# A hybrid diffusion step on one core: a new order for late loads, weight splits, query evictions and the first conv products

## The chip, the core and the metric

One core of a Trainium2 chip runs the whole step. TensorE (PE) multiplies and transposes; VectorE (DVE), ScalarE (ACT) and GpSimd (POOL) do the rest; SyncE (SP) issues nearly all DMAs. The metric is the device time of one execution in microseconds (us): the median of several runs, lower is better.

## The reference

One layer, for 512 latent tokens and 128 context tokens of width 1024, all in float32. Cut to what matters here:

```
mod = silu(cond) @ w_ada + b_ada                     # six parts: sh1 sc1 g1 sh2 sc2 g2
h = rms(x, norm_mix) * (1 + sc1) + sh1
q, k, v, gb, gc, u = split(h @ w_in)                 # 512, 128, 128, 512, 512, 512 columns
q, k = rms per head of 64; latent tokens get rotary positions
attn = softmax(q k^T / 8) v                          # latent queries: 128 cached keys and 512 latent keys in one softmax;
                                                     # context queries: the 128 context keys
y_conv = gb * conv3(gc * u)
x = x + g1 * (concat(rms(attn), rms(y_conv)) @ w_out)
x = x + g2 * ((silu(gate) * up) @ w_down)            # gate, up = split(h2 @ w_gate_up), h2 the second modulated norm
```

The outputs are both token sets and the context's keys and values.

## The kernel before

Every float32 matrix product is three products of split operands: a value is rounded to a high part ("hi", `wh`, `hH`) and the rest is kept as a low part ("lo", `wl`, `hL`); `mm3` issues hi*hi, hi*lo and lo*hi. Splitting a weight tile of 128x1024 takes one ACT instruction for the high part and one DVE instruction for the low part.

**First stage, an order written out by hand.** `P1SEQ` is a string of steps. DVE, ACT, POOL, SP and PE each execute their share of its instructions in the order of the string (each engine by itself; an engine waits only where it needs another's result). Eight rounds k = 0 to 7 go over the eight blocks of 128 of the model width. The letters:

- `rT`, `sT`, `xT`: sum of squares and the inverse root (POOL), scaling, and PE transposes of token tile T (T = 4 is the context); `eTix` evicts half a transposed tile on ACT (`a`) or DVE (`d`).
- `ak`, `bk`, `mk`: the products that give sc1 and sh1 of block k (line 385, from `af` tiles of w_ada), their copy from PSUM (DVE, line 430), and a small product (line 437) whose evictions on DVE give the scale and shift `modA`, `modB`.
- `hk0`, `hk1`: the modulated block `hF`, rounded to `hH` and `hL`, for latent and context tokens.
- `qkT`: the query products of block k and token tile T, three PE instructions.
- `w`, `l`: the ACT and the DVE half of the split of the next loaded w_in tile (lines 526 and 533).
- `c`: constants; `d`: dummy products; `p` (`rows2_load`): five small DMAs on POOL with gains and conv weights; `v1`: a PE transpose of those rows; `R` (`rope_tables`): two DMAs of 128 KB on POOL with the rotary tables, and POOL products for them.

`LOADS` gives SP's order in this stage: `x` a token tile, `A` the four 256 KB loads of w_ada for one block (`af`, buffers for two blocks), `W` the next 512 KB tile of w_in (`wf`, three buffers; the split results have four). `wf` tiles come in the order of `plan`: four for queries, two for keys and values, then the conv tiles for gc, u and gb of each of four column groups, between which lie the w_ada tiles (`aw`) that later stages need.

After the string come two DMAs of the cached keys and values (`ck`, `cv`, 64 KB each) and five copies of the query sums out of PSUM (`qraw`): the context's on DVE, the latent tiles' on ACT. These are not in the hand-written order; a planner with a cost model places them and everything in the next stages on ACT, DVE, POOL and SP. PE's order stays as the program states it.

**Second stage, phase 1.** `SEQ` is the order of PE's work: `kT` key and value products of tile T (`kv_mm`, 24 PE instructions and the per-head norm `head_norm`), `c0` splits the cached keys and values, `CT`/`KT` transpose split keys, `qT`/`QT` norm and transpose queries, `a`, `t`, `o` are the context's attention (scores, transposes, output), `Sn.h`, `Tn.g`, `On.g` the same for 16 units of latent attention, `r` sums of squares. `F1` runs one filler step: 84 steps, in fixed order, of the four conv column groups (six steps each for gc, u and gb, of nine or six PE instructions) and of the rest of the modulation (`ada`). `W(key)` loads ahead: it issues the loads up to a few places past the tile that it is asked for.

**Later stages** (output projection, feed-forward) are not touched.

Of the kernel before, what the change touches and what calls it, by code (L numbers as in the profile page):

```python
# [9 lines left out]
F32 = mybir.dt.float32  # L10
F32R = mybir.dt.float32r
AF = mybir.ActivationFunctionType
# [3 lines left out]
P = 128  # L16
# [3 lines left out]
NT = 5  # L20
TOK = NT * P
CTX = 4
HD = 64
NH = 8
NKV = 2
# [5 lines left out]
EPS = 1e-6  # L31
CG = 32
P1SEQ = ('d8 r0 s0 x0 r1 s1 r2 e00d x1 s2 e01d r3 v0 d4 x2 s3 e20a a0 e10d b0 e11d e21d x3 m0 d4 w e30a h00y l n0 '
# [4 lines left out]
XB = 3  # L38
SEQ = ('k1 c0 q4 k4 C0 k0 K4 Q4 q0 a0 F1 k2 a1 K0 t0 k3 t1 o0 K1 F1 Q0 o1 K2 F1 K3 F1 S0.0 F1 F1 S0.1 '
# [10 lines left out]
GCUT = [0, 6, 12, 17, 22]  # L50
GB = 3
SOP = [20, 0]
# [2 lines left out]
FEND = 2  # L55
AOP = 9
NPLAIN = 2
QEV = '00001'
PPO = ''
RSP = 0  # L60
G2P = -300
# [23 lines left out]
AHEAD = 3  # L85
OSQ = 2
AFB = 4
LOADS = 'xxxxAWxAAWAAWAAAWWWW'
O_Q, O_K, O_GB, O_GC, O_U = 0, 512, 768, 1280, 1792


def build(ctx, tc, x_prompt, x_sample, c, cache_k, cache_v, c_ctx, norm_mix, norm_ffn, w_ada, b_ada,
# [3 lines left out]
    act, dve, pool, pe, sp = nc.scalar, nc.vector, nc.gpsimd, nc.tensor, nc.sync  # L96
# [16 lines left out]
    def close_pool(name):  # L113
        pools[name][0].__exit__(None, None, None)
# [5 lines left out]
    def T(tag, shape, dt=F32, bufs=1):  # L120
        seq[0] += 1
        return pools[where.get(tag, "A")][1].tile(list(shape), dt, tag=tag, bufs=bufs, name=f"{tag}_{seq[0]}")

    def PB(shape=(P, 512), dt=F32, tag="t"):
        seq[0] += 1
        if kept.get(tag):
            w = kept[tag].pop()
            n = 1
            for y in shape[1:]:
                n *= y  # L130
            w = w[:, :n] if tag != "s" else w
            if tag != "s" and len(shape) > 2:
                names = "abc"[:len(shape) - 1]
                w = w.rearrange("p (" + " ".join(names) + ") -> p " + " ".join(names), **dict(zip(names, shape[1:])))
            return w
        return pools["psum"][1].tile(list(shape), dt, tag=tag, bufs=pbufs[tag], name=f"p{tag}_{seq[0]}")
# [52 lines left out]
    def plan(key, src, ph=0, ring="w", gain=None):  # L189
        place[key] = len(order)  # L190
        order.append([key, src, ph, ring, gain, None])
# [60 lines left out]
    def load_next(later=False):  # L252
        load(order[stream_at[0]], later)
        stream_at[0] += 1
# [19 lines left out]
    ada_steps = [(sec, j, h) for sec, j in ADA for h in range(4)]  # L274
    for n, (off, ct) in enumerate(CONV + [(None, 0)]):
        if off is not None:
            plan(("conv", off, ct), wi[:, :, off + ct * P:off + (ct + 1) * P])
        for sec, j, h in ada_steps[2 * n:2 * n + 2 if off is not None else None]:
            col = sec * D + j * 512
            plan(("ada", sec, j, h), wa[:, 2 * h:2 * h + 2, col:col + 512], 1, "a")  # L280
    for j in range(2):
# [17 lines left out]
    for gi, grp in enumerate(GROUPS):  # L299
# [5 lines left out]
        for j in range(2):  # L305
            for i0 in range(0, len(grp), 2):
                n = len(grp[i0:i0 + 2])
# [37 lines left out]
    def x_load():  # L345
        xt = T("x", (P, D), F32, NT)
        sp.dma_start(xt, x_dram[len(xs)])
        xs.append(xt)

    def ada1_next(n):  # L350
        for _ in range(n):
            next(loads, None)
# [5 lines left out]
    pre_order.__enter__()  # L358
    for a in LOADS:
        if a == "A":  # L360
            ada1_next(3)
        elif a == "W":
            load_next(True)
        else:
            x_load()
    ones = T("ones", (P, P))
    dve.memset(ones, 1.0)
    neghalf = T("neghalf", (P, 16))
# [132 lines left out]
    qacc = [PB(tag="c")]  # L501
# [40 lines left out]
    def rows2_load():  # L542
        for nm, g in (("q", q_norm), ("k", k_norm)):
            pool.dma_start(gain_rows[nm], g[0].partition_broadcast(P))
        pool.dma_start(rows2[0:4, :], attn_out_norm[0].rearrange("(r q) -> r q", q=P))
        pool.dma_start(rows2[4:8, :], conv_out_norm[0].rearrange("(r q) -> r q", q=P))
        pool.dma_start(rows2[8:20, :], conv_w[0].rearrange("w (r q) -> (w r) q", q=P))
# [3 lines left out]
    def rope_tables():  # L551

        rt = T("oz", (P, 2, NL, HD))
        rc, rs_ = rt[:, 0], rt[:, 1]
        pool.dma_start(rc, rope_c.rearrange("(t p) d -> p t d", p=P))
        pool.dma_start(rs_, rope_s.rearrange("(t p) d -> p t d", p=P))
        for nm in "qk":
            gb_ = gain_rows[nm]
            tab = T("tab", (P, 2, NL, HD), F32, 2)
            cg, sg = tab[:, 0], tab[:, 1]  # L560
            pool.tensor_tensor(cg, rc, gb_.unsqueeze(1).to_broadcast([P, NL, HD]), ALU.mult)
            s4 = sg.rearrange("p t (a b c) -> p t a b c", a=2, b=2)
            r4 = rs_.rearrange("p t (a b c) -> p t a b c", a=2, b=2)
            g4 = gb_.rearrange("p (a b c) -> p a b c", a=2, b=2)
            for b in range(2):
                for a in range(2):
                    pool.tensor_tensor(s4[:, :, a, b], r4[:, :, a, b],
                                       g4[:, a, 1 - b].unsqueeze(1).to_broadcast([P, NL, 16]), ALU.mult)
            gains.append(gb_)
            tabs.append((cg, sg))  # L570

    steps = {"r": x_norm, "s": x_scale, "c": late_consts, "w": w_hi, "l": w_lo, "p": lambda i: rows2_load(), "x": xT_do,
             "v": lambda i: (vec_do, vec2_do)[i](), "m": ada1_mod, "a": ada1_mm, "b": ada1_res, "d": spin,
             "n": h_rest, "R": lambda i: rope_tables()}
    in_pre[0] = True
    for x in P1SEQ.split():
        k = int(x[1:2] or 0)
# [7 lines left out]
            steps[x[0]](k)  # L585
    pre_order.__exit__(None, None, None)
    in_pre[0] = False
    ck = T("ck", (P, NKV, HD))
    sp.dma_start(ck, cache_k[0, 0])
    cv = T("cv", (P, NKV, HD))  # L590
    sp.dma_start(cv, cache_v[0, 0])
    qraw = [None] * NT
    for t in (CTX, 0, 1, 2, 3):
        qraw[t] = T("of", (P, 512), F32, NT)
        if QEV[t] == '1':
            dve.tensor_copy(qraw[t], qacc[t])
        else:
            act.activation(qraw[t], qacc[t], AF.Copy)
    close_pool("B0")
    open_pool("B2", "left", "vt KA KB VS qT pr ph pl osq c25 aw es")  # L600
    phase[0] = 1
# [203 lines left out]
    of = [None] * NT  # L805
# [137 lines left out]
    def rms_of(t):  # L943
        if t == CTX or t >= 0:
# [5 lines left out]
             "a": ctx_s, "t": ctx_t, "o": ctx_o, "r": att_rms}  # L950
    for x in SEQ.split():
        if "." in x:
            n, i = (int(y) for y in x[1:].split("."))
# [113 lines left out]
    for j in range(2):  # L1067
        cols = slice(j * 512, (j + 1) * 512)
        for n, t in enumerate(TORD):
            cc = 1 if t == CTX else 0  # L1070
            c0 = t * P + (2 if t == CTX else 0)
# [229 lines left out]


tile_hymba = with_exitstack(build)

_INS = ["x_prompt", "x_sample", "c", "cache_k", "cache_v", "c_ctx", "norm_mix", "norm_ffn", "w_ada", "b_ada",
# [44 lines left out]
```

## Time and profile before

| | |
|---|---|
| Median of three runs | 761.21 us (760.87 to 762.34) |
| Profiled execution | 763.84 us, of which the span of instructions 762.1 us |
| PE, DVE, ACT, POOL busy | 742.6, 553.9, 368.0, 43.8 us |
| Mean granted PE clock | 0.995 |
| HBM traffic | 79.68 MB read, 2.75 MB written |
| First stage | up to about 63 us |
| Phase 1 | about 63 to 272 us |

Lines of the profile read: start, duration (us), engine, source line, operation, written tile <- read tiles, shapes, count, and in brackets the idle time before it and what ended it. "Waits" lines read: who waited, for whom, us in total, times, longest. The chain lists start, duration and what held up the end. Windows list the busy time of each engine in a stretch, then the clock granted to PE (1.00 is full), the DMA engines' mean share and GB/s.

### The profile page before, as it was taken

Reading aid. Unit: us, or ns where it says so; the run is one execution under the profiler, and the core shown is the slowest. Engines: PE = TensorE matmul, PEld = TensorE weight load, DVE = VectorE, ACT = ScalarE, POOL = GpSimd, SP = SyncE. Lnnn points to the kernel's source line nnn. Section 1 sums busy time; section 2 is a strip of 40 time slices with the busy share of each in tenths; the row PEclk is TensorE's granted clock in tenths of the full one; section 3 lists DMA queues with packets and bytes.
Section 4 is the critical chain, followed back from the end, with each engine's and each line's share of the span. In section 5 each row is a group of like instructions: output and inputs, shape, how many; then the busy total and the mean of one; then the engine's idle time right before and its main releaser. Section 6 shows DMA issues by size and latency. Waiting matters only on the chain.

```text
span 762.1 us, 11916 instructions
## 1 busy us (share of the span) xinstructions
PE 742.6 (97%) x4612; PEld 666.7 (87%) x4612; DVE 553.9 (73%) x1005; ACT 368.0 (48%) x713; POOL 43.8 (6%) x75
## 2 busy tenths in 40 slices
PE   7899999999999999999999999999999999999997
PEld 5578888989999887899998789998889998899986
DVE  5456997676666798779979678884577866788653
ACT  5336867666656434765652135553125541255410
POOL 2401300111000110100000000000000000000000
PEclk9999999999999999999999999999999999999999
DMA  9966133522432463031335223233113132122312
GB/s 290 289 199 196 36 118 91 171 94 90 156 108 90 132 245 115 1 111 56 89 106 180 83 60 107 69 99 112 54 55 108 60 111 82 57 87 81 111 56 83
DMA packets 101389, 84.52 MB, mean 111 GB/s; under 512 B 3502, under 2 KB 81650, under 8 KB 101332
## 3 DMA queue, kind: packets, MB, share of 16 engines
q1 hardware_dynamic: 100980, 83.39, 35.5%
q8 instruction: 36, 0.59, 0.3%
q0 software_dynamic: 352, 0.37, 0.2%
q14 instruction: 21, 0.17, 0.1%
HBM read 79.68 MB, written 2.75 MB: 108 GB/s over the span
## 4 chain that ended last, share of the span: by engine, by line
PE 84%; DVE 6%; DMA 5%; ACT 2%; issue 1%; SPq 0%; POOL 0%; DVEq 0%; ACTq 0%
PE pf L157 17%; PE pf L156 17%; PE pf L155 17%; PE pc L703 3%; PE pc L705 3%; PE pc L704 3%; PE po L860 2%; PE ps L817 2%; PE pc L385 2%; PE ph L155 2%; PE ph L157 2%; PE ph L156 2%; PE pt L843 2%; DMA af<-in_w_ada_dram 2%; DMA es<-t 1%
## 5 line engine op out<-in xcount | busy, mean ns | idle before, releaser
L151 ACT ACTIVATE wh<-wf 128x512 fp32r<-128x512 f32 (+1 forms) x69 | 56.6, 821 | 85.6 <-PE pf L157 62.0
L157 PE MATMUL pf<-wh,gT 128*128 128x512 f32 (+1 forms) x225 | 88.3, 393 | 0.0
L156 PE MATMUL pf<-wl,gT 128*128 128x512 f32 (+1 forms) x225 | 87.7, 390 | 0.0
L155 PE MATMUL pf<-wh,gT 128*128 128x512 f32 (+1 forms) x225 | 87.6, 389 | 0.0
L152 DVE TENSOR_TENSOR wl<-wf,wh 128x1024 fp32r<-128x1024 f32 (+1 forms) x35 | 40.6, 1161 | 28.7 <-ACT wh L151 23.6
L703 PE MATMUL pc<-hH,wh 128*128 128x320 f32 x192 | 61.1, 318 | 0.0
L705 PE MATMUL pc<-hH,wl 128*128 128x320 f32 x192 | 59.4, 309 | 0.0
L704 PE MATMUL pc<-hL,wh 128*128 128x320 f32 x192 | 59.3, 309 | 0.0
L156 PEld LDWEIGHTS pf<-wl,gT 128*128 128x128 f32 x225 | 42.2, 188 | 10.3 <-DVE wl L152 0.2
L155 PEld LDWEIGHTS pf<-wh,gT 128*128 128x128 f32 x225 | 42.2, 188 | 9.8 <-ACT wh L151 0.2
L155 PE MATMUL pf<-T,wh 128*128 128x320 f32 x160 | 49.6, 310 | 0.9 <-ACT u L1180 0.5
L157 PEld LDWEIGHTS pf<-wh,gT 128*128 128x128 f32 x225 | 42.3, 188 | 9.4
L155 PE MATMUL pf<-T,wl 128*128 128x320 f32 x160 | 49.4, 309 | 0.0
L156 PE MATMUL pf<-T,wl 128*128 128x320 f32 x160 | 49.4, 309 | 0.0
L157 PE MATMUL pf<-T,wh 128*128 128x320 f32 x160 | 49.4, 309 | 0.0
L156 PE MATMUL pf<-T,wh 128*128 128x320 f32 x160 | 49.4, 309 | 0.0
L157 PE MATMUL pf<-T,wl 128*128 128x320 f32 x160 | 49.4, 309 | 0.0
L155 PE MATMUL pf<-B,wl 128*128 128x320 f32 x152 | 47.1, 310 | 0.0
L157 PE MATMUL pf<-B,wl 128*128 128x320 f32 x152 | 47.0, 309 | 0.0
L156 PE MATMUL pf<-B,wl 128*128 128x320 f32 x152 | 46.9, 309 | 0.0
L1259 DVE TENSOR_TENSOR dm<-pf,g 128x512 f32<-128x512 f32 (+1 forms) x41 | 27.7, 675 | 23.4 <-PE pf L157 23.3
L155 PE MATMUL pf<-B,wh 128*128 128x320 f32 x136 | 42.2, 310 | 1.5 <-DVE cu L1209 1.5
(304 smaller groups left out, 2046.5 us busy)
## 6 DMA issues: line engine op xcount, KB each, us to landing
wf<-in_w_gate_up_dram SPq DMA_DIRECT2D x44, 512.0 KB, 3.9
aw<-in_w_ada_dram SPq DMA_DIRECT2D x24, 512.0 KB, 4.5
wf<-in_w_down_dram SPq DMA_DIRECT2D x20, 512.0 KB, 3.4
wf<-in_w_in_dram SPq DMA_DIRECT2D x18, 512.0 KB, 5.7
af<-in_w_ada_dram SPq DMA_DIRECT2D x32, 256.0 KB, 6.7
x<-in_x_sample_dram SPq DMA_DIRECT2D x8, 512.0 KB, 6.1
wf<-in_w_out_dram SPq DMA_DIRECT2D x8, 512.0 KB, 4.3
wf<-in_w_ada_dram SPq DMA_DIRECT2D x8, 512.0 KB, 3.7
```

What stands on the lines that cost most here:

```text
L151: act.activation(hi, src, AF.Copy)
L152: dve.tensor_tensor(lo, src, f32(hi), ALU.subtract)
L155: pe.matmul(out, lh, rh, start=start, stop=False, skip_group_check=more)
L156: pe.matmul(out, lh, rl, start=False, stop=False, skip_group_check=more)
L157: pe.matmul(out, ll, rh, start=False, stop=stop, skip_group_check=more)
L385: pe.matmul(out[CG * g:CG * (g + 1)], cp[:, k], w, start=(k < 4), stop=(k >= KD - 4), skip_group_check=True)
L703: pe.matmul(acc, wh[:, k], hH[k][:, c0:c0 + n], start=(k == 0), stop=False)
L704: pe.matmul(acc, wh[:, k], hL[k][:, c0:c0 + n], start=False, stop=False)
L705: pe.matmul(acc, wl[:, k], hH[k][:, c0:c0 + n], start=False, stop=(k == KD - 1))
L817: pe.matmul(s2[:, g, :320], q, kk[:, v, P + g * 320:P + (g + 1) * 320], start=(i == 0), stop=(i == 1))
L843: pe.transpose(tp[:, i, h], u[3][h][:, kt * P:(kt + 1) * P], ident)
L1259: dve.tensor_tensor(dm, ps[:, :n], g2[cc][:, oc], ALU.mult)
```

## The change

- The DMAs of `ck` and `cv` move into the hand-written order, behind all of `LOADS`, on SP.
- `LOADS` gets an eighth `W`: the first u tile of the conv is loaded and split in the first stage too. In `plan` the w_ada tiles move one conv tile later, so that this tile is next.
- In `P1SEQ` the splits `w l` from the fourth on come earlier: the fourth in round 6 ahead of `q51` (it was behind `b7`), the fifth ahead of `q54` (it was behind `q61`), the sixth behind `q61`, the seventh behind `q64`, and the new eighth at the end.
- `a3 b3` move behind `q13 q14`, and `q20` ahead of `m3`. `p0` moves from round 1 to round 2, `R` from round 4 to round 5, `v1` from round 2 to the end of round 5.
- The five query copies become steps `E0` to `E4` between the last query products, in the hand-written order; before, the context's copy stood first in the program.
- In `SEQ` one filler moves between `K4` and `Q4`, others move ahead around `Q0`, `K2`, `K3` and `S0`, and one each is taken out behind `T9.1` and `T14.1`. The number of fillers is the same, 84.

```
-         'r4 q01 e31d s4 p0 q02 a1 x4 b1 e40d m1 h01x h10 q00 a2 b2 h11 q04 m2 w e41a q03 l q10 h20 q11 q12 h21 a3 b3 q13 q14 '
-         'm3 h30 h31 q20 q21 a4 b4 q22 q23 c0 q24 v1 m4 h40 h41 R q30 q31 a5 b5 w l q32 q33 q34 '
-         'm5 h50 h51 q40 q41 a6 b6 q42 q43 q44 m6 h60 h61 q50 q51 a7 b7 w l q52 q53 q54 '
-         'm7 h70 h71 q60 q61 w l q62 q63 q64 w l w l q70 q71 q72 q73 q74')
+         'r4 q01 e31d s4 q02 a1 x4 b1 e40d m1 h01x h10 q00 a2 b2 h11 q04 m2 w e41a q03 l q10 h20 q11 q12 h21 q13 q14 a3 b3 '
+         'q20 m3 h30 h31 q21 a4 b4 q22 q23 c0 p0 q24 m4 h40 h41 q30 q31 a5 b5 w l q32 q33 q34 '
+         'm5 h50 h51 q40 q41 a6 b6 q42 q43 R q44 m6 h60 h61 q50 w l q51 a7 b7 q52 q53 w l q54 v1 '
+         'm7 h70 h71 q60 q61 w l q62 q63 q64 w l q70 E0 q71 E1 q72 E2 q73 E3 q74 E4 w l')
...
-SEQ = ('k1 c0 q4 k4 C0 k0 K4 Q4 q0 a0 F1 k2 a1 K0 t0 k3 t1 o0 K1 F1 Q0 o1 K2 F1 K3 F1 S0.0 F1 F1 S0.1 '
+SEQ = ('k1 c0 q4 k4 C0 k0 K4 F1 Q4 q0 a0 F1 k2 a1 K0 t0 k3 t1 o0 K1 F1 Q0 o1 F1 K2 F1 K3 F1 F1 S0.0 F1 S0.1 '
...
-       'T8.1 F1 S9.1 T8.2 O8.0 F1 O8.1 S10.0 F1 F1 T9.0 O8.2 T9.1 F1 F1 F1 O9.0 T9.2 S10.1 F1 r1 O9.1 '
+       'T8.1 F1 S9.1 T8.2 O8.0 F1 O8.1 S10.0 F1 F1 T9.0 O8.2 T9.1 F1 F1 O9.0 T9.2 S10.1 F1 r1 O9.1 '
...
-       'T14.1 F1 F1 F1 T14.2 F1 F1 O14.0 O14.1 T15.0 F1 O14.2 F1 T15.1 T15.2 F1 F1 O15.0 O15.1 F1 O15.2')
+       'T14.1 F1 F1 T14.2 F1 F1 O14.0 O14.1 T15.0 F1 O14.2 F1 T15.1 T15.2 F1 F1 O15.0 O15.1 F1 O15.2')
...
-LOADS = 'xxxxAWxAAWAAWAAAWWWW'
+LOADS = 'xxxxAWxAAWAAWAAAWWWWW'
...
-        for sec, j, h in ada_steps[2 * n:2 * n + 2 if off is not None else None]:
+        for sec, j, h in ada_steps[2 * n - 2:2 * n if off is not None else None] if n else ():
...
+    ck, cv = (T(x, (P, NKV, HD)) for x in ("ck", "cv"))
+    sp.dma_start(ck, cache_k[0, 0])
+    sp.dma_start(cv, cache_v[0, 0])
...
+    def q_evict(t):
+        qraw[t] = T("of", (P, 512), F32, NT)
+        if t == CTX:
+            dve.tensor_copy(qraw[t], qacc[t])
+        else:
+            act.activation(qraw[t], qacc[t], AF.Copy)
```

The lines behind the loop over `P1SEQ` that issued `ck`, `cv` and the five copies go away with `QEV`, and the step table gets `"E": q_evict`.

More of the change, by code (lines that the diff above doesn't have):

```diff
@@ L57 @@
 NPLAIN = 2
-QEV = '00001'
 PPO = ''
@@ L570, in rope_tables @@
             tabs.append((cg, sg))
+    qraw = [None] * NT
+    def q_evict(t):
[4 more added lines that the diff above has]
+            act.activation(qraw[t], qacc[t], AF.Copy)
     steps = {"r": x_norm, "s": x_scale, "c": late_consts, "w": w_hi, "l": w_lo, "p": lambda i: rows2_load(), "x": xT_do,
              "v": lambda i: (vec_do, vec2_do)[i](), "m": ada1_mod, "a": ada1_mm, "b": ada1_res, "d": spin,
-             "n": h_rest, "R": lambda i: rope_tables()}
+             "n": h_rest, "E": q_evict, "R": lambda i: rope_tables()}
     in_pre[0] = True
@@ L587, in build @@
     in_pre[0] = False
[L588 to L598, printed above, removed]
     close_pool("B0")
```

## The prediction

> **What bounds the kernel now.** First the page's head, then who TensorE (PE) waited for, then the stretches those waits lie in.
>
> ```profile
> span 762.1 us, 11916 instructions
> PE 742.6 (97%) x4612; PEld 666.7 (87%) x4612; DVE 553.9 (73%) x1005; ACT 368.0 (48%) x713; POOL 43.8 (6%) x75
> ```
> ```profile
> PE pc L385 <- DMA af<-in_w_ada_dram: 2.4, 1, 2.4
> PE pt L647 <- ACT osq L639: 1.6, 1, 1.6
> ...
> PE pt L683 <- ACT qT L684: 1.0, 1, 1.0
> PE ps L817 <- ACT pr L825: 0.8, 1, 0.8
> ```
> PE is busy for 742.6 of 762.1 us. The change adds and removes no product, so it can only win PE's idle time or the clock. Four large waits lie where it edits. The windows (PE, PEld, DVE, ACT, POOL busy, granted clock, DMA share, GB/s) show what the first two cost besides:
>
> ```profile
> 27.50:31.00 3.50, 1.20 (x11) 0.31 (x9) 1.16 (x3) 0.74 (x1) 1.57 (x4) 1.00 1.14 268
> 31.00:34.40 3.40, 3.15 (x13) 1.98 (x14) 0.42 (x1) 0.00 (x0) 2.30 (x7) 0.50 1.05 300
> ...
> 68.50:71.90 3.40, 1.52 (x12) 1.19 (x11) 2.62 (x9) 1.80 (x6) 2.52 (x2) 1.00 0.56 157
> 71.90:75.30 3.40, 3.40 (x19) 3.40 (x18) 2.96 (x10) 1.58 (x5) 0.75 (x2) 0.51 0.10 31
> ```
> ```profile
> 86.00:92.00 6.00, 5.43 (x43) 4.78 (x42) 5.80 (x19) 5.97 (x20) 1.25 (x2) 1.00 0.19 53
> ...
> 98.00:104.00 6.00, 5.21 (x35) 3.91 (x35) 5.38 (x11) 4.49 (x9) 0.00 (x0) 1.00 0.56 152
> ...
> 110.00:272.00 162.00, 161.44 (x1152) 146.16 (x1151) 112.35 (x222) 100.34 (x202) 15.63 (x25) 1.00 0.37 118
> ```
> After each of the two long waits PE runs one stretch at half clock (0.50, 0.51). In 110 to 272 us PE idles 0.56 us, so a gain made before 105 us is carried to the end. In 86 to 104 VectorE (DVE) is itself over 90% busy (5.80 and 5.38 of 6): what is won before it may be capped there.
>
> **Change, part 1: the fourth round of the first stage (27 to 41 us).**
>
> ```profile
> 22.05 9.07 DMA af<-in_w_ada_dram
> ```
> ```profile
> 27.43 0.40 PE L156 MATMUL ps<-wl,hH 128*128 128x512 f32 x1
> 27.66 0.40 PE L157 MATMUL ps<-wh,hL 128*128 128x512 f32 x1
> ...
> 31.25 1.08 PE L385 MATMUL pc<-af,cp 128*32 128x256 f32 x8 [2.37 <-DMA af<-in_w_ada_dram]
> ...
> 35.10 0.47 PE L155 MATMUL ps<-wh,hH 128*128 128x512 f32 x1
> ```
> ```profile
> 19.05 0.47 SPq L589 DMA_DIRECT2D ck<-in_cache_k_dram  x1
> 19.57 0.43 SPq L591 DMA_DIRECT2D cv<-in_cache_v_dram  x1
> 20.13 9.74 SPq L324 DMA_DIRECT2D af<-in_w_ada_dram  x8
> ```
> *Loads.* The cached keys and values stand on SP's queue just ahead of the modulation weights that a3 waits for. They are 2 x 64 KB = 131 kB; at the 268 to 300 GB/s of the windows that is 0.45 us. So the last a3 load lands at 31.12 - 0.45 = 30.67. Bounds: 0 (SP's buffers come free no sooner) and 1.08 (the issue time 19.05 to 20.13).
> *a3 behind q13 q14.* Six products start 0.23 apart (27.43, 27.66): 1.40 us of work that needs only round 1, moved into the 2.37 us wait. Idle left: 2.37 - 1.40 - 0.45 = 0.52, a gain of 1.85 (1.4 to 2.37).
> *Clock.* From 31.25 to 35.10, 3.85 us, PE does half of a3, q13, q14 and m3 at half clock; at the warm spacing this is about 0.5 + 0.4 of switching + 1.4 + 0.35 = 2.65. With q13 q14 ahead, the window 27.5 to 31 holds 1.20 + 1.40 = 2.6 busy of 3.5 and I take it to stay warm: 1.2 (0 to 1.3). Sum 3.05; I take 3.0, bounds 1.4 and 3.7. Next late is the load of round 4, some 1 MB or 3.6 us behind a3's at those rates, at 34.3 at the latest; PE wants it at about 33.4, and its first half comes sooner: up to 0.5 of the 3.7 may go there.
> *p0, R, v1.* p0 and R issue seven DMAs, all on POOL.
>
> ```profile
> 21.91 0.79 POOL L555 DMA_DIRECT2D oz<-rope_c_dram  x1
> ```
> R stood behind h41 in the order, yet POOL issued it at 21.91: each engine follows the order by itself, and nothing but the r steps stands before p0 on POOL. Moving p0 and R leaves POOL's order as it is: nothing changes, and their 336 KB stay in the way of a3's load (bounds 0 and -1.1 us, their bytes at 300 GB/s). v1 is one transpose moved; PE pays it in either place: 0.
>
> **Part 2: splits one round sooner (52 to 60 us).**
>
> ```profile
> 53.00 1.04 ACT L526 ACTIVATE wh<-wf 128x1024 fp32r<-128x1024 f32 x1
> ...
> 53.87 0.42 DVE L430 COPY res<-pc 128x256 f32<-128x256 f32 x1
> 54.20 1.22 DVE L533 TENSOR_TENSOR wl<-wf,wh 128x1024 fp32r<-128x1024 f32 x1
> ...
> 56.65 0.82 ACT L474 ACTIVATE hF<-xT,modB,modA 128x512 f32<-128x512 f32 x1 [2.60 <-DVE modB L412]
> ...
> 58.26 0.82 DVE L152 TENSOR_TENSOR hL<-hF,hH 128x640 fp32r<-128x640 f32 x1 [1.27 <-ACT hH L151]
> ...
> 60.06 0.40 PE L157 MATMUL ps<-wh,hL 128*128 128x512 f32 x1
> ```
> In the last round the third split's DVE half now precedes b7, and a fourth split precedes m7. DVE has done them by 54.1 + 1.22 + 0.42 + 1.22 = 56.95, so m7's evictions, and hF7 with them (56.65), start about 0.8 later, and hL7 ends near 59.9 in place of 59.08. The cover is q60 to q64, 15 products or 3.5 us; the first use of hL7 is q70's third product, at 60.06 and itself moved by some 0.3. On ScalarE (ACT) the extra half-split (1.04, as at 53.00) lies in its 2.60 us idle time. Cost 0.2; 0.9 if the cover fails; more only if that weight lands late, since hF7 now stands behind it on ACT.
> The sixth to eighth split move too. The eighth, of the first U weights, now is a step before phase 1, and SP loads it sooner because the fifth frees its buffer sooner:
>
> ```profile
> 60.47 4.98 DMA wf<-in_w_in_dram
> ```
> ```profile
> 66.62 1.23 DVE L152 TENSOR_TENSOR wl<-wf,wh 128x1024 fp32r<-128x1024 f32 x1 [2.64 <-ACT wh L151]
> 67.76 0.28 DVE L612 TENSOR_REDUCE hq_ss<-ph 128x2 f32<-128x128 f32 x1
> 70.58 0.37 PE L647 MATMUL pt<-identr,osq 128*128 128x128 f32 x2 [1.64 <-ACT osq L639]
> ...
> 74.71 0.42 DVE L640 TENSOR_TENSOR osq<-pr,osq 128x256 fp32r<-128x256 f32 x1
> ```
> Its load goes out at about 57 in place of 60.47 (on the old time scale), lands before ACT is through the query evictions, and its DVE half ends near 66.0, not 67.85. The key norm then starts when k1 is done, near 66.7 in place of 67.76: 1.0 us off the 1.64 us wait at C0 (0 to 1.87 with the 0.23 behind it). Evictions as steps E0 to E4 are the same five instructions on the same engines (the context one on DVE, as now): 0. The cached values land some 6 us after about 58, the keys before them, against a use at 69: 0, and 1 for 1 if later than that.
>
> **Part 3: conv products among the transposes (63 to 105 us).**
>
> ```profile
> 64.16 0.28 PE L155 MATMUL pc<-wh,hH 128*128 128x256 f32 x1
> 64.28 0.28 PE L156 MATMUL pc<-wl,hH 128*128 128x256 f32 x1
> ...
> 72.30 0.42 PE L155 MATMUL pc<-wh,hH 128*128 128x256 f32 x1
> 72.51 0.41 PE L156 MATMUL pc<-wl,hH 128*128 128x256 f32 x1
> ...
> 77.62 0.54 PE L683 MATMUL pt<-identr,qT 128*128 128x128 f32 x4 [1.01 <-ACT qT L684]
> ...
> 79.02 0.31 PE L703 MATMUL pc<-hH,wh 128*128 128x320 f32 x1
> ...
> 80.34 0.28 PE L155 MATMUL pc<-wh,hH 128*128 128x256 f32 x1
> ```
> *K4 F1 Q4.* One F1 is 1.32 us (79.02 to 80.34); it covers the 1.01 us wait inside Q4: 1.0 (0 to 1.0).
> *Clock.* Of k0's products 16 start 0.21 apart in place of 0.12: 1.5 us. With C0's wait down to 0.65 the stretch stays warm: 1.5 (0 to 1.5).
> *Given back.* k0 starts at 70.58 - 1.0 + 0.8 for C0's transposes and ends 24 x 0.12 later, near 73.2 (old scale). K4 needs the split context key, which DVE finished at 75.13 (74.71 + 0.42) on the same chain as the key norm; moved by the norm's 1.1 it is there at 74.05. A new wait of 0.85 (0 to 1.5) at K4, which the half clock had hidden.
> *The other three F1 moves* exchange places in a stretch where DVE is the fuller engine; the 0.8 us wait at S0.1 now has one filler ahead of it, not two, but a softmax that starts sooner: 0.15 (-0.9 to 0.8). The waits at C0, K4, S0.1, Q4 together: 1.0 + 1.0 + 1.5 - 0.85 + 0.15 = 2.8, and 0.2 for the second wait at C0: 3.0 (0.5 to 4.9). The fillers taken out at T9.1 and T14.1 leave two there, 1.9 us or more; cost 0.3 (0 to 1.2).
>
> **Sum.** 3.0 - 0.2 + 3.0 - 0.3 = 5.5 us. The profiled execution took 763.84 (its span 762.1), so 758.3 there; the median of the runs is 761.21, 2.63 lower, so 755.7.
>
> [...] The windows show half clock after stretches with 1.20 of 3.5 and 1.52 of 3.4 us busy. [...]
>
> **Rivals.**
> 1. *DVE caps phase 1.* The 3.0 of parts 2 and 3 shrinks to about 0.5, since DVE is over 90% busy from 86 to 104. For it: those rows. Against it: DVE itself starts about 1 us sooner at 67.76 and idles 2.64 before 66.62. 761.21 - 3.0 + 0.2 - 0.5 + 0.3 = 758.2.
> 2. *The load wait moves* from a3 to a4 and a5: part 1 gives the 0.45 of bytes and half the clock loss, 1.0. For: the DMA share is full through 34. Against: the load of round 4 lands at worst 0.9 after PE wants it. 757.7.
> 3. *The clock does not follow the gaps:* the half-clock stretches come anyway. Minus 1.2 and 1.5 of the sum: 758.4. The windows speak against it.
> 4. *No change:* the order on chip is not the written one where it matters, as for p0 and R, and gains of part 1 are lost in phase 1: 761.2.
> 5. *Slower:* the planner, fed with other due times, puts 1.22 us weight splits ahead of softmax steps on DVE between 83 and 104. It decides from 2.8 us on, so that part 1 is eaten: three splits, 3.7 us, and a half-clock stretch behind such a wait, 1.5. 761.21 - 2.8 + 5.2 = 763.6. Against it: one split stands there in most rounds already.
>
> **How the numbers follow.** Forecast 0.52; rivals 1: 0.17, 2: 0.10, 3: 0.05, 4: 0.08, 5: 0.08. About 0.2% (1.5 us) is what a measurement tells from no change: under 759.7 is faster, over 762.7 slower. Faster 0.84, same 0.08, slower 0.08. All bounds met at the good end would give 3.7 + 4.9 - 0 = 8.6 or 752.6; range 753.0 to 759.7, which takes in rivals 1 to 3 and leaves out 4 and 5. The forecast's own range is 753.5 to 757.5.
>
> **What would show it.** Part 1: the wait of L385 on af under 1 us, and no granted clock of 0.5 before 60. Part 2: the eighth split done before the key norm's first DVE step; L647's wait under 1 us; ck issued after the last w_in load of the first stage; rope_c still issued near 22. Part 3: no 1.0 us wait inside Q4, a new one at K4, full clock in k0. Wrong if the af wait only moves, if PE waits at q70, or if new waits over 1 us stand between 83 and 105.

## The result and the profile after

The change made the kernel slower: 767.95 us median (766.52 to 770.75) beside 762.24 (760.87 to 763.83), ratio 1.008, 95% interval 1.0053 to 1.0107. The forecast was 755.7. The profiled execution took 768.41, its span 766.6, 4.5 more than before.

Whom TensorE (PE) waited for between 50 and 272 us, the changed kernel (us in total, times, longest):

```profile
PE ps L817 <- ACT pr L825: 2.6, 2, 2.1
PE ps L154 <- ACT of L581: 1.5, 2, 0.8
PE po L860 <- ACT t L867: 1.2, 1, 1.2
PE pt L683 <- DVE pl L151: 0.7, 1, 0.7
PE pt L647 <- ACT osq L639: 0.6, 2, 0.3
```

The waits that were to go are gone: none on `af`, C0's two (L647) are 0.3 us at most where one was 1.64, and the one inside Q4 on `qT` is gone. Two larger ones are new (1.5 us on `of` in round 7, 1.2 us on `t` near 147 us), the one at S0.1 (L817) has grown from 0.8 to 2.1, and another query transpose waits 0.7 us on `pl`, 0.2 before. Stretches of the changed kernel (PE, PEld, DVE, ACT, POOL busy, granted clock, DMA share, GB/s):

```profile
27.50:31.00 3.50, 3.50 (x21) 2.55 (x25) 2.40 (x5) 1.87 (x3) 0.70 (x1) 1.00 1.14 262
31.00:34.40 3.40, 3.31 (x34) 1.79 (x23) 1.48 (x5) 0.81 (x1) 3.30 (x10) 1.00 1.13 319
...
71.90:75.30 3.40, 3.03 (x25) 2.67 (x24) 3.33 (x13) 2.37 (x7) 0.74 (x2) 1.00 0.13 41
...
72.00:112.00 40.00, 35.61 (x253) 32.59 (x252) 33.10 (x85) 27.20 (x70) 5.93 (x9) 0.96 0.25 77
112.00:272.00 160.00, 157.46 (x1122) 141.17 (x1122) 108.73 (x215) 98.85 (x201) 13.65 (x24) 1.00 0.35 111
```

And the last two stretches of the kernel before:

```profile
72.00:112.00 40.00, 37.50 (x273) 34.41 (x271) 36.04 (x95) 29.68 (x76) 6.62 (x10) 0.96 0.26 76
112.00:272.00 160.00, 159.44 (x1137) 144.17 (x1136) 110.75 (x219) 98.97 (x199) 15.63 (x25) 1.00 0.37 119
```

The half clock near 31 and 72 is gone (0.50 and 0.51 before, 1.00 in the rows above). But PE now idles 4.4 us in 72 to 112 (2.5 before), a half-clock stretch still among them (0.51 from 101.30 us), and 2.5 us in 112 to 272 (0.6 before). VectorE (DVE) is less busy there, not more: 33.1 us of 40 beside 36.0. When PE begins certain work, by the timelines of the profiled executions (us; e1 to e18 are the experiments below, S0.0 comes three fillers later in the new order than in the old):

| | last group of a7 | k1 | C0 | S0.0 | output projection |
|---|---|---|---|---|---|
| before | 52.44 | 63.09 | 70.58 | 95.63 | 258.88 |
| after | 49.43 | 62.49 | 68.65 | 95.99 | 263.20 |
| e1, part 1 alone | 49.81 | 60.46 | 67.99 | 92.00 | 258.04 |
| e2, after with the old SEQ | 49.27 | 62.28 | 68.45 | 92.47 | 255.65 |
| e3, after, evictions moved | 49.38 | 60.40 | 66.57 | 93.90 | 259.10 |
| e4, before with the new SEQ | 52.55 | 63.19 | 70.00 | 97.34 | 262.59 |
| e5, e3 with the old SEQ | 49.53 | 60.55 | 66.72 | 90.74 | 253.93 |
| e17, new to S0.1, then old | 49.71 | 60.72 | 66.90 | 94.23 | 258.41 |
| e18, old to S0.1, then new | 49.31 | 60.32 | 66.50 | 92.04 | 261.22 |

Each row is one execution. That of e1 took 762.69, the longest of its twelve (median 759.84), with half clock from 227 to 231 us (0.50 in the 3.41 us from 227.30).

**Round 7 eats most of part 1.** The gain is 3.0 us at a7 and 0.6 at k1. The timelines of SP, ScalarE (ACT) and PE, changed kernel:

```profile
54.82 0.82 SPq L367 DMA_DIRECT2D cv<-in_cache_v_dram  x1
...
57.84 0.60 ACT L581 ACTIVATE of<-ps 128x512 f32<-128x512 f32 x1
59.64 0.31 ACT L150 ACTIVATE VS<-cv 128x128 fp32r<-128x128 f32 x1 [1.21 <-DMA cv<-in_cache_v_dram]
59.86 1.07 ACT L581 ACTIVATE of<-ps 128x512 f32<-128x512 f32 x2
...
58.49 0.50 PE L154 MATMUL ps<-wh,hH 128*128 128x512 f32 x1 [0.69 <-ACT of L581]
60.98 0.50 PE L154 MATMUL ps<-wh,hH 128*128 128x512 f32 x1 [0.83 <-ACT of L581]
```

The query sums q0 and q1 share one PSUM tile (128x2x512), q2 and q3 another. `q70 E0 q71` lets E0 read the tile that q71 writes next, so q71 waits for E0, and q73 for E2. Between E0 and E1 the planner put the split of the cached values, which waits 1.21 us for `cv`, issued behind all loads of the stage.

**S0.1.** DVE and PE, changed kernel:

```profile
96.01 0.42 DVE L881 TENSOR_TENSOR of<-t,es 64x256 f32<-64x256 f32 x1 [0.32 <-DMA es<-t]
96.83 0.42 DVE L882 TENSOR_TENSOR of<-t,es 64x256 f32<-64x256 f32 x1 [0.40 <-DMA es<-t]
97.28 1.23 DVE L151 TENSOR_TENSOR wl<-wf,wh 128x1024 fp32r<-128x1024 f32 x1
98.43 0.82 DVE L821 TENSOR_REDUCE nm<-ps 128x1 f32<-128x640 f32 x1
...
100.22 0.56 PE L817 MATMUL ps<-KA,qT 128*128 128x320 f32 x2 [2.06 <-ACT pr L825]
```

The scores of S0.0 are done near 96.85; two additions and a weight split stand ahead of their maximum (`nm`), which starts 1.6 us late. PE waits 2.06 us and then runs at half clock (0.51 in the row 101.30 to 104.71, further down).

### The profile page after: what moved, and what is told of

It reads as the page before. It is cut to its first block, busy times and chain, and to the rows that moved or that the text cites. A ratio compares the mean times of both kernels' runs of the same rounds, so it can differ in the third digit from the quotient of the medians.

```text
span 766.6 us, 11914 instructions
## 1 busy us (share of the span) xinstructions
PE 746.0 (97%) x4612; PEld 668.3 (87%) x4612; DVE 554.0 (72%) x1005; ACT 368.2 (48%) x713; POOL 43.7 (6%) x75
## 4 chain that ended last, share of the span: by engine, by line
PE 83%; DVE 7%; ACT 4%; DMA 3%; issue 2%; POOL 1%; SPq 0%; DVEq 0%; POOLq 0%
PE pf L156 17%; PE pf L155 17%; PE pf L154 17%; PE pc L703 3%; PE pc L704 3%; PE pc L705 3%; PE po L860 3%; PE ph L154 2%; PE ph L156 2%; PE ph L155 2%; PE ps L817 2%; PE pc L387 2%; PE pt L843 2%; DMA es<-t 1%; PE ps L154 1%
```

## Experiments

Each ran beside the kernel before, in five rounds; ratios are to that kernel, with 95% intervals. What differs by less than about 1 us counts as the same.

**Which part.** e1 is the kernel before with part 1 alone (`a3 b3 q13 q14` to `q13 q14 a3 b3`, `ck` and `cv` behind the loop over `LOADS`). e2 is the changed kernel with SEQ undone, e4 the kernel before with the new SEQ alone. e3 is the changed kernel with

```
-q70 E0 q71 E1 q72 E2 q73 E3 q74 E4 w l
+q70 q71 E0 E1 q72 q73 E2 E3 q74 E4 w l
```

> The kernel before with part 1 alone: q13 q14 ahead of a3, and the cached keys and values behind the last hand-ordered load. Everything later is the order of before. Theory A (the new written order of phase 1 loses the time, by the order that it gives VectorE): part 1's 3.0 us are kept to the end, 759.2 where before is 762.2, ratio 0.996; no wait over 1 us behind 83 us. Theory B (whatever is won ahead of phase 1 is eaten there, VectorE being its bound): 761.5 to 762.2. Theory C (the late cached values cost it): cv lands about 3 us after its last use can begin, 1 to 2 us lost at its split, 760.5.

Measured 759.84, ratio 0.996 (0.9945 to 0.9974): 2.8 us faster. The cached values behind the queue cost nothing here: no instruction waits for `cv` in this trace.

> The changed kernel with the phase-1 order of before (SEQ undone; parts 1 and 2 and the load list kept). Theory A: the S0.1 wait of 2.06 us, the half clock behind it and the 1.24 us wait near 147 us go; what is left is part 1 less the 2.05 us of round 7 and a shorter wait at C0: 760.2 where before is 762.2, ratio 0.997. Rival (the load list or the sooner splits re-dealt phase 1): the 2 us wait at S0.1 stays and the time stays over 766, ratio 1.005 or more.

Measured 761.53, ratio 0.9982 (0.9968 to 0.9995): 1.3 over the first theory's 760.2, far from its rival's 766. The waits at S0.1 (0.5 now) and near 147 us (none) went with SEQ.

> The changed kernel with 'q70 q71 E0 E1 q72 q73 E2 E3 q74 E4': no product follows into a PSUM tile that an eviction still reads. If the 2.05 us lost in round 7 are the two waits of q71 and q73 on E0 and E2 (0.69 and 0.83): both go, k1 starts 1.5 us sooner, and the time is 1.5 us under the changed kernel's, 766.4, unless S0.1 gives it back (then 767.9). If the late cached values are the cause, k1 starts as late as before, since ScalarE still waits for cv among the evictions.

Measured 764.33, ratio 1.0027 (1.0015 to 1.004). k1 starts 2.1 us sooner and the time falls by 3.6, more than the 1.5 expected: with S0.1's wait at 1.6 no half clock follows it in this trace (1.00 in 92 to 112 us). The executions with a mean clock of 1.00 took 766.52 and 767.31 in the changed kernel and 763.78 to 764.45 in e3, so at full clock the move is worth about 2.8. `cv` lands as late as ever; its split now stands behind E1, where nobody waits.

> The kernel before with the new phase-1 order alone (SEQ of the change, nothing else). Theory A: the order itself puts two context additions and a weight split ahead of the first maximum, so the 2 us wait at S0.1, the half clock and the wait near 147 us all come; 5 to 8 us slower than before, 768.5. Rival (they come from the sooner arrival of everything, or from the load list): within 2 us of before, and faster by the wait at Q4.

Measured 767.93, ratio 1.0072 (1.0046 to 1.0097). SEQ alone is 5.3 us slower, so neither the sooner splits nor the load list is needed for the loss.

**What in SEQ.** e5 undoes SEQ in e3. e6 is e5 with `K4 Q4` made `K4 F1 Q4` and one F1 less at T9.1. e8 has `o1 K2` made `o1 F1 K2` besides, paid for at T14.1. e7 is e3 with the first maximum, the second context additions and one weight split in a hand order on DVE:

```
+            with tc.manual_schedule(engines={mybir.EngineType.DVE}):
+                dve.tensor_reduce(nm, s_in, AX.XY, ALU.max, negate=True)
+                for do in held: do()
```

> Parts 1 and 2 with the phase-1 order of before and the evictions each put behind the last product into their two-bank PSUM tile. The waits of q71 and q73 go (1.5 us) and k1 starts near 60.4 as in the run with the moved evictions; the key transposes start near 66.5, against 67.99 with part 1 alone, since the eighth split is a step. Theory: 1.5 to 2.1 us under the run with the old order (761.5), so 759.7, and 1.4 us under part 1 alone (759.8), so 758.5; together 758.5 to 759.7. Rival (VectorE is the bound of phase 1 and eats what comes sooner): 761 or more.

Measured 759.48, ratio 0.997 (0.9953 to 0.9986): as expected against e2, but no better than part 1 alone (1.4 better was expected), though C0 comes 1.3 us sooner.

> The same, with one filler moved: 'K4 F1 Q4', paid for at T9.1. This is the one move of the new order whose gain the forecast put at 1.0 us (the wait inside Q4). VectorE's order now has both context additions ahead of the first maximum, but no second weight split between them and it, and ScalarE's order near the 1.24 us wait is that of the old order. If the second split and the missing filler between S0.0 and S0.1 make the S0.1 wait: it stays under 0.8 here, the 1.24 us wait does not come, the Q4 wait goes, and the time is 0 to 1 us under the kernel without the move. If the additions alone make it: S0.1 waits 1 us or more and the time is 1 us or more over it.

Measured 763.03, ratio 1.0015 (1.0003 to 1.0026). One filler moved costs 3.5 us. S0.1's longest wait stays at 0.8, and the 1.24 us wait does not come, as the first branch has it, but not its time; the second branch has the time and not the wait. What waits now is S0.0, DVE and PE of e6:

```profile
92.41 1.22 DVE L151 TENSOR_TENSOR wl<-wf,wh 128x1024 fp32r<-128x1024 f32 x1
...
93.88 0.42 DVE L650 CAST KB<-pt 128x256 fp32r<-128x256 f32 x1
...
94.36 0.41 PE L817 MATMUL ps<-KB,qT 128*128 128x320 f32 x1 [1.03 <-DVE KB L650]
```

> The changed kernel with the evictions moved (764.3, S0.1 wait 1.63 us), and VectorE told by hand to take the first maximum ahead of the second context additions and of the weight split of the GB products; PE's order is untouched. If VectorE's order makes the S0.1 wait: the maximum starts as S0.0 ends, 1.1 us sooner, the wait falls to 0.5 and the time by 1.1, to 763.2; the 1.24 us wait near 147 us stays. If the missing filler between S0.0 and S0.1 makes it: the wait stays at 1.6 and the time at 764.3.

Measured 767.85, ratio 1.0068 (1.005 to 1.0086): slower by 3.5. Waits of PE in e7 (lines shifted by the edit):

```profile
PE ph L154 <- ACT rs L763: 1.9, 1, 1.9
PE pt L856 <- DVE pl L151: 1.5, 2, 0.9
...
PE ps L822 <- ACT pr L838: 0.5, 1, 0.5
```

DVE's order did make the S0.1 wait: it fell from 1.6 to 0.5 with PE's order untouched. The time was more than given back. S0.0 starts 1.4 us later than in e3, and the 1.9 us wait is a new one: the first product of the output projection waits for the eviction of the last filler's sums (L763 here, L758 in the changed kernel), and in this trace half clock follows from 263 to 267 us (0.50 in the 3.41 us from 263.20). Neither the changed kernel nor e3 has that wait. e10, e14, e16 and e18 have it too (1.93 us in each), and their times have to be read with it; it is shown with e18.

> The kernel with parts 1 and 2 and the moved evictions, with two of the three filler moves: 'K4 F1 Q4' and 'o1 F1 K2', paid for at T9.1 and T14.1; 'S0.0 F1 F1 S0.1' as before. From here on ScalarE's order near the context of unit 5 is that of the changed kernel (a weight split, an exponential, two splits and a copy ahead of the eviction t). If that order makes the 1.24 us wait: it comes here and not with 'K4 F1 Q4' alone; S0.1 waits under 0.8; the time lies 1 to 2 us over the kernel with 'K4 F1 Q4' alone, 760.5. If the 1.24 us wait comes of the pace of PE: it is absent in both or there in both.

Measured 764.11, ratio 1.0026 (1.0012 to 1.004), with S0.1 at 0.5, with the 1.24 us wait, and 1.1 us over e6: the step and its mechanism as expected. The time is 3.6 over the 760.5 expected, because its base, e6, already was.

**Long splits as the cause?** e9 is e3 with one eviction, `t` of unit 3, on DVE. e10, e11, e12 are e3, e6, e5 with DVE's half of each conv split in two steps. e13 to e16 nearly take the splits away, in the old order (e13, e15) and the new (e14, e16):

```
-                split(wh, wl, wf)
+                act.activation(wh[:, :a], wf[:, :a], AF.Copy)            # e13, e14; [:, :n] in e15, e16
+                dve.tensor_tensor(wl[:, :n], wf[:, :n], f32(wh[:, :n]), ALU.subtract)   # n = 1 for conv
...
-                pe.matmul(acc, wl[:, k], hH[k][:, c0:c0 + n], ...
+                pe.matmul(acc, wl[:, 0], hH[k][:, c0:c0 + n], ...
```

> The changed kernel with the evictions moved (764.3), and one eviction, t of unit 3, on VectorE instead of ScalarE, where it stood behind a weight split, an exponential, two splits and a copy while PE waited 1.24 us. VectorE takes it ahead of the same weight's second half. If ScalarE's order made the wait and it is carried to the end: the wait falls to 0.4 or less (the splits ph and pl come 0.4 to 0.7 us after) and the time by 0.8 to 1.2, 763.3. If the time is given back by later waits of the same kind: 764.3.

Measured 764.21, ratio 1.0028 (1.0015 to 1.004). PE's idle time in 112 to 272 fell from 2.4 to 1.5 us, as the wait should, but the median did not; 0.8 us is at the edge of what it resolves. Left open.

> The changed kernel with the evictions moved, and VectorE's half of each conv weight split in two steps of 512 columns (about 0.68 us each in place of 1.22), so that a step that becomes ready behind one waits at most 0.68. In VectorE's order the first maximum now has neither the second context addition's split nor a whole weight split right ahead of it. If long splits ahead of short urgent steps are what the new order costs: the S0.1 wait falls from 1.6 to 0.5, and the time by 1 to 2 us, 762.8, in spite of 0.14 us more work for each split. If VectorE's whole load is the bound: slower by the added work, up to 2 us, 766.

Measured 768.83, ratio 1.0087 (1.0069 to 1.0105): over both branches. S0.1's wait falls to 0.7, near the first branch, but 1.93 us at the output projection and 1.3 us on the cast of a key tile are new.

> The same halving in the kernel with 'K4 F1 Q4' alone (763.0). There the cast of the last key tile stood behind a whole weight split and S0.0 waited 1.03 us for it. Long splits as the cause: that wait falls to 0.5 or less, the time by 1 us or more, 762.0 or less. VectorE's whole load as the bound: 764.

Measured 764.04, ratio 1.0025 (1.0014 to 1.0037): 1.0 over e6, the second branch. S0.0's wait on the cast is gone, as the first branch had it, and the time is not.

> The same halving in the kernel with parts 1 and 2, the moved evictions and the phase-1 order of before (759.5). Its first maximum stands behind a whole split, by luck without harm but for 0.5 us at S0.1. Long splits as the cause: little to win here, S0.1 at 0.2 or less, 758.5 to 759.5. VectorE's whole load as the bound: 760 to 761.5. An order that is re-dealt to the worse: over 761.5.

Measured 762.04, ratio 0.9988 (0.9972 to 1.0004): 2.5 slower, the third branch. New waits, 0.9 us on a key cast and 1.2 on `pl`, stand elsewhere, and a half-clock stretch from 74 to 78 us (0.50).

> Leaves work out: VectorE's half of a conv weight split makes one of eight blocks (128 columns in place of 1024), and the third product of each conv step takes that block eight times; products, loads and ScalarE's half are as before. Parts 1 and 2, moved evictions, phase-1 order of before (759.5 with the whole splits). It takes some ten splits of 1.1 us off VectorE. If VectorE's splits hold PE up even in the old order (0.5 at S0.1 and little else): 758.5 to 759.5. It is the base for the next run.

Measured 761.86, ratio 0.9987 (0.9975 to 0.9999): with less work it is 2.4 us slower than e5, against the expectation.

> Leaves the same work out, with the new phase-1 order (764.3 with the whole splits, 4.9 over the old order). If VectorE's weight splits ahead of what PE waits for are what the new order costs, the difference to the old order shrinks from 4.9 to 1.5 or less (the 1.24 us wait on ScalarE's order stays): 760.5 or less. If the new order's loss has other grounds (ScalarE's order, or PE's own order with less between S0.0 and S0.1): the difference stays at 3 us or more, 762 or more.

Measured 767.51, ratio 1.0054 (1.0035 to 1.0073): 5.6 over e13, or 3.7 without the 1.93 us at the output projection. The wait at S0.1 stays at 1.5, behind the two additions and a split of only 0.29, so the theory falls. Two stretches, e13 and e14:

```profile
72.00:112.00 40.00, 35.98 (x265) 32.62 (x265) 32.87 (x88) 28.64 (x73) 5.81 (x9) 1.00 0.25 75
112.00:272.00 160.00, 159.07 (x1133) 143.42 (x1132) 104.74 (x219) 97.56 (x197) 14.63 (x25) 1.00 0.38 124
```
```profile
72.00:112.00 40.00, 36.08 (x270) 32.95 (x272) 31.46 (x83) 28.54 (x72) 5.50 (x9) 1.00 0.25 73
112.00:272.00 160.00, 156.28 (x1106) 140.02 (x1102) 103.97 (x218) 97.51 (x197) 14.16 (x25) 1.00 0.38 122
```

Up to 112 us PE idles alike, 4.0 and 3.9 us; behind it 0.9 in the old order and 3.7 in the new, 1.8 of it ahead of the output projection. So part of the loss arises far behind the edits.

> Leaves out more: ScalarE's half too makes one block of eight, which all conv products take. Old order. It takes some ten steps of 0.9 us off ScalarE besides. ScalarE is at 75% in this stage, so little changes: 758 to 759.5.

Measured 759.11, ratio 0.9938 (0.9919 to 0.9956), as expected.

> The same left out, with the new order. If weight splits on both engines are the whole of its loss, the 1.24 us wait falls to 0.3 (0.9 us of ScalarE's work goes from in front of it), S0.1 waits 0.7 or less, and the new order is as fast as the old or faster by the 1.0 us of Q4: 757 to 759.5. If the loss is in PE's own order, with one filler less between S0.0 and S0.1 and the 0.7 us waits on pl: it stays 2 us or more over the old order.

Measured 765.2, ratio 1.0029 (1.0015 to 1.0042): 6.1 over e15, or 4.2 without the 1.93 us at the output projection. The waits that were laid to the splits shrink nearly as expected, to 0.7 at S0.1 and 0.5 near 147 us, and the time does not follow: most of the 4.9 that the new order costs with whole splits (e3 against e5) is still there. So the splits make part of these two waits and are not the main cause.

**The filler list.** What PE does while it waits near 147 us, and ACT's order, changed kernel:

```profile
143.78 1.06 ACT L150 ACTIVATE wh<-wf 128x1024 fp32r<-128x1024 f32 x1 [0.64 <-PE pc L704]
144.74 0.78 ACT L825 ACTIVATE pr<-ps,nm 128x640 f32<-128x640 f32 x1
...
145.51 1.07 ACT L150 ACTIVATE ph<-pt 128x512 fp32r<-128x512 f32 x2
146.47 0.45 ACT L717 ACTIVATE c<-pc 128x320 f32<-128x320 f32 x1
146.78 0.40 ACT L867 ACTIVATE t<-po 128x256 f32<-128x256 f32 x1
...
144.93 1.07 PE L387 MATMUL pc<-aw,cp 128*32 128x512 f32 x8
147.24 0.39 PE L860 MATMUL po<-ph,VS 128*128 128x256 f32 x1 [1.24 <-ACT t L867]
```

The F1 between T4.1 and O4.0 is a modulation step (L387). In the old order a conv piece stands in that slot, e5 (its last product and O4.0's first, with no wait):

```profile
137.79 0.31 PE L705 MATMUL pc<-hH,wl 128*128 128x320 f32 x1
137.94 0.28 PE L860 MATMUL po<-ph,VS 128*128 128x256 f32 x1
```

F1 takes the next piece of one fixed list. Two fillers sooner, and one each taken out at T9.1 and T14.1, give every slot from S0.1 to T9.1 a piece two places on, with its loads, splits and evictions. e17 has the new order up to S0.1 and pays back at once; e18 has the old order and goes two ahead right behind S0.1. From S1.0 on, ACT's and DVE's orders in e17 soon become those of e5, in e18 those of e3:

```
e17, on e3:  -q1 F1 F1 S1.0 F1        +q1 S1.0 F1             T9.1 and T14.1 with three F1 again
e18, on e5:  -q1 F1 F1 S1.0 F1        +q1 F1 F1 F1 F1 S1.0 F1 T9.1 and T14.1 with two F1
```

> New theory, after the weight splits fell as the cause: the F1 steps draw the conv and modulation products from one list, in turn. Two fillers sooner, and paid back only at T9.1 and T14.1, every filler slot between S0.1 and T9.1 gets another piece of that list (a modulation step where a conv step stood, a piece with an eviction behind it where one without stood), and the waits of the long stretch come from that. This kernel has the new order up to S0.1 with the moved evictions (764.3), but gives the two fillers back right there ('q1 S1.0 F1' for 'q1 F1 F1 S1.0 F1') and keeps three at T9.1 and T14.1, so that from S1.0 on all engines' orders are those of the old order. Theory: no 1.24 us wait, TensorE idles about 0.9 in 112 to 272 us in place of 2.4, and the time falls by 2 to 3, to 761.5 to 762.3; the loss before S1.0 stays. Rival (the loss is made in 72 to 112 alone, by less cover and DVE's order): 764 or more, since two fillers' cover goes at S1.0.

Measured 764.48, ratio 1.0035 (1.0022 to 1.0049).

> The other way round: the old order (759.5) up to S0.1, and then two fillers more ('q1 F1 F1 F1 F1 S1.0 F1'), paid back at T9.1 and T14.1 as in the change, so that from S1.0 on all engines' orders are those of the changed kernel. Theory: the 1.24 us wait near 145 us comes, TensorE idles about 2.4 in 112 to 272 us in place of 0.9, and the time rises by 2 to 3 over the old order, to 761.5 to 762.5, though nothing is moved ahead of S0.1. Rival (the early moves make the loss): no more than 0.5 over the old order.

Measured 766.65, ratio 1.006 (1.0044 to 1.0076). Stretches of e5, e3, e17 and e18, in this order:

```profile
92.00:112.00 20.00, 19.38 (x142) 16.88 (x140) 17.50 (x35) 14.69 (x29) 0.00 (x0) 1.00 0.35 106
112.00:272.00 160.00, 159.10 (x1126) 143.55 (x1119) 111.93 (x220) 96.89 (x196) 16.38 (x26) 1.00 0.40 129
```
```profile
92.00:112.00 20.00, 17.70 (x125) 15.47 (x128) 16.40 (x33) 13.04 (x26) 0.00 (x0) 1.00 0.38 112
112.00:272.00 160.00, 157.58 (x1111) 140.99 (x1104) 108.55 (x216) 97.35 (x197) 15.33 (x25) 1.00 0.37 119
```
```profile
92.00:112.00 20.00, 16.23 (x104) 14.12 (x103) 15.77 (x30) 11.67 (x25) 0.00 (x0) 0.91 0.37 111
112.00:272.00 160.00, 159.54 (x1140) 144.23 (x1138) 110.95 (x220) 98.55 (x199) 15.59 (x25) 1.00 0.37 121
```
```profile
92.00:112.00 20.00, 18.81 (x131) 16.72 (x129) 16.04 (x32) 12.17 (x24) 0.00 (x0) 1.00 0.36 112
112.00:272.00 160.00, 155.82 (x1097) 139.30 (x1096) 108.11 (x214) 96.89 (x197) 14.89 (x25) 0.99 0.37 119
```

PE idles 0.9 us (e5) and 0.5 (e17) behind 112 us with the old alignment, that is, where each slot gets its old piece of the list, and 2.4 (e3) and 4.2 (e18) with the new one. But e18 holds a wait that has no part in the question. ACT and PE of e3, then of e18, at the start of the output projection:

```profile
260.56 0.58 ACT L758 ACTIVATE rs<-pc 128x512 f32<-128x512 f32 x1
259.10 0.40 PE L154 MATMUL ph<-wh,m 128*128 128x512 f32 x1
```
```profile
260.59 0.58 ACT L758 ACTIVATE rs<-pc 128x512 f32<-128x512 f32 x1
257.80 1.07 PE L387 MATMUL pc<-aw,cp 128*32 128x512 f32 x8
261.22 0.80 PE L154 MATMUL ph<-wh,m 128*128 128x512 f32 x1 [1.93 <-ACT rs L758]
```

Both kernels stand at the same step at the same time, and only in e18 does the first product of the projection wait for the eviction `rs`. Perhaps its PSUM tile takes the place of the evicted one there; the traces do not show places, so the reason is open. Without these 1.93 us e18 idles 2.3, as e3 does. In all twenty traces, the wait left out, PE idles 0.5 to 1.3 us behind 112 us in the eight with the old alignment, 2.2 and 2.8 in the two that are one filler ahead (e6, e11), and 1.5 to 2.8 in the ten that are two ahead. So the alignment decides the idle time there, both ways, and the 1.24 us wait comes in e18 and not in e17; it is worth about 1.5 us of idle time.

e18 moves nothing ahead of S0.1 and is 7.2 us slower than e5. Of these, 1.9 are the wait at the projection, and by estimate up to 1.7 the half clock behind it (0.50 in 261.03 to 264.44 us, half of 3.41); the changed kernel has neither. Less both, by estimate, e18 would lie near 763, close to the theory's 761.5 to 762.5 and well over its rival's 760.

Between 92 and 112 us PE idles 0.6 and 1.2 us with the old early moves (e5, e18), 2.3 and 3.8 with the new (e3, e17). The moves are not all of it: e12 and e13 have the old ones and idle 2.1 and 2.3. In e17 the two fillers that cover S0.1 and S1.0 are gone, PE waits 1.8 us twice and falls to half clock (0.51 in the 3.41 us from 101.70), so the total is no better than e3's: the theory's idle time was right there, its time wrong, and 764.48 is what its rival said.

What stays open is, first, how the early loss divides between less cover at S0.1 and DVE's order there: e7 took 1.1 us off the wait by DVE's order alone, and lost it elsewhere. Second, idle time is not all that SEQ costs. From the start of k1 to the output projection, the same products in e5 and in e3:

```profile
60.55:253.93 193.38, 189.66 (x1397) 172.79 (x1396) 140.13 (x307) 125.45 (x272) 20.97 (x34) 1.00 0.37 114
60.40:259.10 198.70, 191.68 (x1398) 173.37 (x1397) 139.72 (x307) 125.96 (x272) 20.68 (x34) 1.00 0.35 111
```

Of the 5.3 us between them, 3.3 are PE's idle time (3.7 and 7.0); the other 2.0 lie inside what counts as busy, at the same clock, and are not placed. Nor is all of the 8.8 us between the profiled spans of e18 (766.2) and e5 (757.4): idle time in 60 to 272 us gives 3.8, the wait at the projection among it, and two half-clock stretches, near 73 and 261 us (0.50 in both; e5 has 1.00 from 60 to 272), by estimate up to 3.4.

## Why the prediction was wrong

- **Part 1, 3.0: right** in mechanism and size. a7 ends 3.0 us sooner, the half clock is gone (0.50 in 31.00 to 34.40 before, 1.00 now), and alone it is worth 2.8 us.
- **Part 2, "Evictions as steps E0 to E4 are the same five instructions ...: 0": this step failed.** The same instructions between products of one PSUM tile cost 2.1 us at k1, and 3.6 of the time (2.8 at full clock). For "The cached values ...: 0" the load was timed against its use at 69 us, and not against what the planner would queue behind its split on ACT, which waits 1.21 us; no run tests that share by itself. The eighth split did what it was to do: C0's wait is 0.3. But e5, whose C0 comes 1.3 us sooner than e1's, ends no sooner; where that gain goes is open.
- **Part 3, the filler moves: the step that failed most.** Of the 3.0 less 0.3, SEQ's own terms are Q4 (1.0), the other three moves (0.15) and T9.1 and T14.1 (-0.3), a gain of 0.85; the rest (C0, the clock in k0, K4) comes with part 2's eighth split. The price of an F1 was taken where it was put (1.0 at Q4) and where it was taken away ("leave two there ...; cost 0.3"). But the 43 slots from S0.1 to T9.1 all get another piece of the list. Measured, SEQ costs 4.9 us (e3 against e5), 5.3 (e4) or 6.4 (the changed kernel against e2), and the Q4 move alone costs 3.5. The traces place 3.3 of e3's 5.3 as idle time of PE: some 1.5 behind 112 us, by the alignment, and the rest ahead of it, at S0.1 above all.
- **The clock in k0, 1.5,** came as said, and by luck: e1 waits 1.7 us at C0 and has no half clock behind it either (1.00), and e12 and e18, which wait 0.3 there, have a half-clock stretch from 74.4 and 73.3 us (0.50 in both). The small wait at K4 came (0.25, forecast 0.85).
- **That "a gain made before 105 us is carried to the end"** was read from 0.56 us of idle time. That row holds for one alignment of the list only; with the new one the stretch idles 2.5.
- Together: from the 5.5 forecast as a gain to the 5.7 measured as a loss it is 11.2 us. The evictions are 3.6 of it. SEQ is 5.7: 4.9 lost and 0.85 not won. The last 1.9 is what parts 1 and 2 promised without either (3.0 - 0.2 + 1.0 + 0.2 + 1.5 - 0.85 = 4.65) and e5 does not show: 759.48 is 2.8 under 762.24.
- **Rival 5** had the side, the place (83 to 104 us) and the marks, a split ahead of the maximum and a half-clock stretch behind the wait. Its mechanism makes part of one wait, 2.06 us in place of 0.8, and not most of the loss: with the splits nearly gone 3.7 and 4.2 us of the loss stay (e14, e16, less the wait at the projection). Rival 1 fell, as DVE is less busy than before where PE waits; rival 2, as no wait on `af` is left; rival 4, as the time rose. Rival 3, that the clock does not follow the gaps, is half right: half clock came behind one wait at S0.1 (2.06 us, the changed kernel) and not behind another (1.6 us, e3), as the last section shows.

## What to carry to other kernels

Where filler work comes from one ordered list, moving one filler re-deals every slot up to where it is paid back: price each slot between, or pay it back at once and count the cover that this takes away (e17). A drain of one half of a PSUM tile between products into its two halves was a wait both times here (0.69 and 0.83 us). Before a run is read as a test of one cause, look through all of its waits: five of these runs carry 1.9 us at a place that the question did not touch. Where a planner orders the other engines, most edits in this stage moved the time by 1 to 5 us, even one that only took work away (e13), so a forecast there needs a term of that size in its range, and a stretch that hardly idles is no promise that it stays so.

## The hardware, as the runs showed it

Two rows of the changed kernel around S0.1's wait:

```profile
97.89:101.30 3.41, 1.35 (x9) 1.09 (x9) 2.60 (x6) 1.33 (x4) 0.00 (x0) 0.98 1.05 365
101.30:104.71 3.41, 3.41 (x15) 3.41 (x14) 1.99 (x4) 1.71 (x3) 0.00 (x0) 0.51 0.63 176
```

In windows of 0.2 us, between 18 and 275 us, e3 shows no half clock, and nine traces show it in eleven stretches: two each in the kernel before and e18, one each in the changed kernel, e1, e4, e7, e11, e12 and e17. Each lasts 3.4 us, at 0.50. In the 3.41 us ahead of a stretch PE was busy for 1.01 us (the kernel before, ahead of 31.10) to 2.36 (e18, ahead of 73.30; 2.24 in e1, ahead of 227.30). But 2.07 us of 3.42 in e1 (from 66.87) and 2.18 in the changed kernel (from 145.67) were followed by a clock of 1.00, so PE's busy time alone does not tell in these traces where half clock comes; what does is not shown. A wait may or may not cost up to 1.7 us by it (an estimate, half of 3.4): the 1.6 us at S0.1 in e3 had a clock of 1.00 behind them, the 2.06 in the changed kernel 0.51. The clock differs between executions of one program, too: e7's took 766.34 to 767.05 us at a mean clock of 1.00 (three) and 768.64 to 769.45 at 0.996 (three).
